# Causal attention in a hybrid block: key tiles in groups of four with the values one group later, and denominators from a sum in two float32r parts

## The chip, the cores and the metric

The kernel runs as one program on one core of a Trainium2 chip. The metric is the time of one execution on the device in microseconds (us). The names of the engines are those of the profile: PE is the matrix engine (PEld its weight loads), DVE the vector engine, ACT the scalar engine, POOL the general-purpose engine, SP the engine whose queue starts nearly all transfers (DMA) here.

## What is computed

One layer of a streaming encoder over 16 learned tokens and 2048 frames of width 1024, in float32. Three groups of heads read the same normalised input through one projection: a gated linear recurrence, eight heads of forgetting attention with 64 columns each, and a second recurrence (four heads, chunks of 64 frames). Their outputs are joined, projected, added to the input, and a gated feed-forward layer follows. The change concerns the attention alone:

```python
log_f = jax.nn.log_sigmoid(f_logit + f_bias)
c = jnp.cumsum(log_f, axis=1).transpose(0, 2, 1)
...
s = einsum('bhqd,bhkd->bhqk', qb, kh) + (cb[..., :, None] - c[..., None, :])
s = jnp.where(kpos[None, :] <= qpos[:, None], s, -jnp.inf)
p = jax.nn.softmax(s, axis=-1)
o = jnp.einsum('bhqk,bhkd->bhqd', p, vh)
```

## The kernel before

The program goes through the input projection with the recurrences beside it, then the attention (class `Attn`), the output projection (`w_out_tile`, tile `pswo`), and the feed-forward layer (tiles `psu`, then `psd`). All of the code's instructions are put in order for each engine by a scheduler that runs when the kernel is built; each engine then works through its own list strictly in that order, and so does SP's queue of transfers. The order of an engine is therefore no copy of the order of the code, but the code's order is what the scheduler starts from, and `issue_after` and `add_manual_dep` bind it.

`Attn.run` works in steps. A step is one head `h` and one block `b` of 512 queries; half 1 takes the blocks 0 and 1 of all heads, half 2 the blocks 2 and 3, so there are 32 steps. The keys of a step are cut into tiles of 128: a step of block b has 4b + 5 tiles (5, 9, 13 or 17), of which four lie on the diagonal and get narrower (512, 400, 272, 144 columns), and one has 16 rows only. For a tile,

- two float32r products make the transposed scores in tile `sc` (lines 623 and 624, two buffers in PSUM),
- ACT takes the exponential into tile `p` (line 626, `NP` = 5 buffers), and on the diagonal POOL masks it (`affine_select`, line 628),
- a product in plain float32 multiplies `p` by the values `v` into `po` (line 635). Two tiles make a pair: the one writes rows 0 to 63 of `po` and the other rows 64 to 127 (`tile_position`), and the first of them is made to wait for both exponentials,
- POOL, and for each fourth tile DVE, adds `p` into `acc` (line 656), one addition after the other; `acc` has two buffers, one for a step.

Before a step's scores, its maxima are needed (`maxima`): up to 20 products into `mx` (line 503), each reduced by DVE (line 506). They are for the step two ahead and are put between the pairs by `fill`, as are the tiles of the output projection that can already be made. At a step's end, `po` is read out (lines 664 to 667). The denominators follow in three parts, 2, 7 and 12 pairs later (`DELAYS`, `tick`): `total` adds the rows of `acc` by a plain float32 product with a column of ones (line 675), ACT writes the sum over row 0 of `acc` (line 676), and SP sends it out and back as a 16 x 32 tile; `invert` takes the reciprocal and sends it out and back again; `scale` multiplies. The eight w_out tiles 9 to 16 need the outputs of half 2's steps, and most of them run after the attention.

`keys` starts the loads of a head's keys and values. In half 2 a head fills one of two sets of buffers.

Of the kernel before, what the change touches and what calls it, by code (L numbers as in the profile page):

```python
# [18 lines left out]
P = 128  # L19
# [296 lines left out]
def attn_consts(core):  # L316
# [16 lines left out]
    core.ones_col = c.tile([P, 1], F32, name="ones_col")  # L333
    nc.vector.memset(core.ones_col[:], 1.0)
# [59 lines left out]
class Attn:  # L394
# [7 lines left out]
    def __init__(self, core, pool, psum, more, scr):  # L402
# [3 lines left out]
        self.clock, self.later, self.serial, self.added = 0, [], 0, 0  # L406

# [46 lines left out]
    def keys(self, h, nt):  # L454
# [20 lines left out]
        nc.sync.dma_start(v1[:, : nt - 1], scr["v"][: n - META, r].rearrange("(j p) d -> p j d", p=P))  # L475
        nc.sync.dma_start(v1[:META, nt - 1], scr["v"][n - META : n, r])
# [120 lines left out]
    def weights(self, h, b, keys, queries, fill):  # L597
# [4 lines left out]

        nc, core, scr = self.nc, self.core, self.scr
# [8 lines left out]
        po = self.psum.tile([P, 512], F32, tag="pv", name=core.n("po"), bufs=1)  # L612
        acc = self.t([P, 512], "acc")
        for jj in range(0, len(kt), 2):
            if jj:
                fill(min(1.0, (jj + 2) / len(kt)))
            self.tick()
            pair = kt[jj : jj + 2]
            ps_, exps = [], []
            for j, rows, c0, mw, mo in pair:  # L620
                w, ks = n - c0, P * j
                ps = self.ps("sc", 2)
                nc.tensor.matmul(ps[:rows, :w], k1[:, ks : ks + rows], q1[:, c0:n], start=True, stop=False)
                nc.tensor.matmul(ps[:rows, :w], k2[:, ks : ks + rows], q2[:, c0:n], start=False, stop=True)  # L624
                p = self.pool.tile([P, 512], F32, tag="p", name=core.n("p"), bufs=self.NP)
                last = nc.scalar.activation(p[:rows, :w], ps[:rows, :w], AF.Exp, bias=bias[:rows, j : j + 1])  # L626
                if mw:
                    last = nc.gpsimd.affine_select(
                        out=p[:rows, :mw], in_=p[:rows, :mw], compare_op=ALU.is_ge, fill=0.0, base=mo,
                        pattern=[[1, mw]], channel_multiplier=-1,  # L630
                    )
                ps_.append(p)
                exps.append(last)
            for i, (p, (j, rows, c0, mw, mo)) in enumerate(zip(ps_, pair)):
                mm = nc.tensor.matmul(
                    po[64 * i : 64 * i + 64, c0:n], v1[:rows, j], p[:rows, : n - c0],
                    start=jj == 0, stop=jj + i + 2 >= len(kt), tile_position=(0, 64 * i),
                )
                self.last = mm
                if i == 0 and len(pair) == 2:  # L640
                    core.tc.add_manual_dep(
                        mm.ins, exps[1].ins.name,
                        mybir.DependencyInfo(mybir.DependencyClass.Sync, mybir.DependencyReason.DATA),
                        reason="both of a pair at the same time",
                    )
            for i, (p, (j, rows, c0, mw, mo)) in enumerate(zip(ps_, pair)):
                if jj == 0 and i == 0:

                    c1 = pair[1][2] if len(pair) == 2 else n
                    if c1:  # L650
                        nc.gpsimd.tensor_copy(acc[:rows, :c1], p[:rows, :c1])
                    continue
# [3 lines left out]
                eng.tensor_tensor(a, ps_[0][:rows, c0:n] if jj == 0 else a, p[:rows, : n - c0], op=ALU.add)  # L656


        while len(self.later) > 8:
            self.later.pop(0)[2]()  # L660

        o, oh = self.t([64, 512], "o", bufs=4), self.t([64, 512], "oh")
        c1 = kt[1][2]
        nc.scalar.activation(oh[:, c1:n], po[64:128, c1:n], AF.Copy)
        if c1:
            nc.scalar.activation(o[:, :c1], po[0:64, :c1], AF.Copy)
        nc.vector.tensor_tensor(o[:, c1:n], po[0:64, c1:n], oh[:, c1:n], op=ALU.add)
        g = n // 16
        dcol = self.t([16, 32], "dcol", bufs=4)
        rows = kt[0][1]  # L670
        rb = []

        def total():
            ps = self.mx()
            nc.tensor.matmul(ps[0:1, :n], core.ones_col[:rows], acc[:rows, :n], start=True, stop=True)
            nc.scalar.activation(acc[0:1, :n], ps[0:1, :n], AF.Copy)
            nc.sync.dma_start(scr["den"][h : h + 1, ts], acc[0:1, :n])
            nc.sync.dma_start(dcol[:, :g], scr["den"][h, ts].rearrange("(p c) -> p c", c=g))

        def invert():  # L680
            rb.append(self.t([64, 512], "rb"))
            nc.vector.reciprocal(dcol[:, :g], dcol[:, :g])
            nc.sync.dma_start(scr["rden"][h, ts].rearrange("(p c) -> p c", c=g), dcol[:, :g])
            nc.sync.dma_start(rb[0][:, :n], scr["rden"][h : h + 1, ts].broadcast_to([64, n]))

        def scale():
            nc.vector.tensor_tensor(o[:, :n], o[:, :n], rb[0][:, :n], op=ALU.mult)
# [1375 lines left out]
```

## Time and profile before

| what | us |
|---|---|
| median of three runs (3157.63 to 3165.91) | 3165.64 |
| the profiled execution, its own time | 3168.61 |
| its span, first to last instruction | 3166.9 |
| input projection with recurrences, to the first scores | about 0 to 927 |
| attention, half 1, with the rest of the recurrences | about 927 to 1210 |
| attention, half 2, with parts of the output projection | about 1210 to 1690 |
| the rest of the output projection | about 1690 to 1800 |
| feed-forward layer | about 1800 to 3167 |

The bounds of the stages are the first and last starts of their instructions in the trace. Of the lines below, a row of a group of instructions gives the line of the code, the engine, the operation, the tiles it writes and reads, the shape and the count; then the busy time and the mean ns of one; then how long the engine stood idle before them, and which engine's work ended that. A row of stretches gives the busy time of each engine in that stretch (with the number of instructions), the granted clock of PE as a share of the full one, the share of the DMA engines and GB/s. PE's products overlap in time: what one costs is the distance from its start to the start of the next.

### The profile page before, as it was taken

To read this page: it belongs to the slowest core of one execution; us is meant where nothing else is said; L and a number is where in the kernel's file an instruction comes from. 1 tells how busy PE (TensorE), PEld (TensorE's weight loads), DVE (VectorE), ACT (ScalarE), POOL (GpSimd) and SP (SyncE) were. 2 spreads that over 40 slices of the span, in tenths; PEclk is the share of its full clock that TensorE was granted. 3 is DMA by queue.
4 is the path that set the end of the run, shared out by engine and by line. 5 is a ranking of instruction groups with operands and counts; after the bars stand their busy time and mean duration, and the time that the engine had idled before them with its cause. 6 is when DMAs were issued, how large, how long until landed. Compare 5 with 4: busy or idle time off the path is not lost. (4 is left out here: it accounts for less than half of the span.)

```text
span 3166.9 us, 52619 instructions
## 1 busy us (share of the span) xinstructions
PE 2955.7 (93%) x18488; PEld 2473.9 (78%) x18488; DVE 2196.1 (69%) x4563; ACT 1446.3 (46%) x2684; POOL 1274.0 (40%) x1426
## 2 busy tenths in 40 slices
PE   6988899999989998999999899999999999999998
PEld 6977788889965554554457699999999999787776
DVE  6147665766677777766657777787778787557777
ACT  3134323444444443434543456666666665324332
POOL 3334334211013444434651235433533334556665
PEclk9989899999987998999999899999999999999999
DMA  6777756643453344444326365555555565535444
GB/s 194 225 235 229 220 181 215 200 125 111 116 126 68 81 100 123 119 109 116 77 61 206 115 190 168 167 173 168 165 165 164 168 189 159 177 103 170 140 160 140
DMA packets 493817, 484.11 MB, mean 153 GB/s; under 512 B 83200, under 2 KB 408010, under 8 KB 487904
## 3 DMA queue, kind: packets, MB, share of 16 engines
q1 hardware_dynamic: 493168, 480.36, 50.8%
q8 instruction: 145, 2.38, 0.3%
q14 instruction: 120, 0.98, 0.1%
q0 software_dynamic: 384, 0.39, 0.0%
HBM read 354.76 MB, written 125.87 MB: 152 GB/s over the span
## 5 line engine op out<-in xcount | busy, mean ns | idle before, releaser
L150 PE MATMUL psu<-xo,uw 128*128 128x344 f32 x1848 | 588.7, 323 | 7.9 <-DVE wx L1413 4.8
L151 PE MATMUL psu<-xo,uw 128*128 128x344 f32 x1848 | 593.7, 322 | 1.0 <-DVE xo L1485 1.0
L152 PE MATMUL psu<-xo,uw 128*128 128x344 f32 x1848 | 583.0, 320 | 0.0
L150 PE MATMUL psp<-xh,wh 128*128 128x384 f32 (+2 forms) x1152 | 386.0, 335 | 0.0
L152 PE MATMUL psp<-xh,wl 128*128 128x384 f32 (+2 forms) x1152 | 382.1, 332 | 3.0 <-DVE wl L145 3.0
L151 PE MATMUL psp<-xl,wh 128*128 128x384 f32 (+2 forms) x1152 | 383.0, 332 | 0.0
L150 PEld LDWEIGHTS psu<-xo,uw 128*128 128x128 f32 x1848 | 347.5, 189 | 9.4 <-DVE wx L1413 5.2
L151 PEld LDWEIGHTS psu<-xo,uw 128*128 128x128 f32 x1848 | 348.9, 189 | 1.3 <-DVE xo L1485 1.3
L152 PEld LDWEIGHTS psu<-xo,uw 128*128 128x128 f32 x1848 | 347.2, 189 | 0.0
L1484 ACT ACTIVATE uw<-uq 128x512 fp32r<-128x512 f32 x462 | 287.0, 627 | 99.1 <-PE psu L152 48.0
L1485 DVE TENSOR_TENSOR uw<-uq,uw 128x512 fp32r<-128x512 f32 x330 | 283.2, 862 | 63.5 <-ACT uw L1484 58.6
L626 ACT ACTIVATE p<-sc,bias 128x512 f32<-128x512 f32 (+4 forms) x352 | 201.1, 592 | 267.8 <-PE sc L624 211.7
L1485 POOL TENSOR_TENSOR uw<-uq,uw 128x512 fp32r<-128x512 f32 x132 | 182.4, 1382 | 267.2 <-ACT uw L1484 233.8
L656 POOL TENSOR_TENSOR acc<-acc,p 128x512 f32<-128x512 f32 (+3 forms) x208 | 226.6, 1090 | 153.2 <-ACT p L626 118.8
L1584 DVE SCALAR_TENSOR_TENSOR uy<-psu,ffn_cols,uy 128x342 f32<-128x342 f32 (+1 forms) x396 | 224.2, 569 | 90.0 <-ACT uy L1582 88.9
L1590 POOL TENSOR_TENSOR uy<-uy,uy 128x342 f32<-128x342 f32 (+1 forms) x132 | 137.0, 1038 | 322.0 <-DVE uy L1584 133.9
L506 DVE TENSOR_REDUCE mc<-mx 128x1 f32<-128x400 f32 (+6 forms) x320 | 172.5, 554 | 93.4 <-PE mx L503 89.2
L152 PEld LDWEIGHTS psp<-xh,wl 128*128 128x128 f32 x1152 | 222.6, 193 | 10.3 <-issue 4.5
L150 PEld LDWEIGHTS psp<-xh,wh 128*128 128x128 f32 x1152 | 222.6, 193 | 8.8 <-issue 6.5
L151 PEld LDWEIGHTS psp<-xl,wh 128*128 128x128 f32 x1152 | 222.6, 193 | 6.5 <-issue 4.6
L1503 POOL TENSOR_TENSOR us<-us 128x512 f32<-128x512 f32 x88 | 131.3, 1492 | 222.3 <-DMA us<-in_ffn_up_dram 197.5
L1484 ACT ACTIVATE fo<-u 128x896 fp32r<-128x896 f32 x88 | 81.1, 922 | 234.3 <-POOL u L1700 117.1
(447 smaller groups left out, 6513.7 us busy)
## 6 DMA issues: line engine op xcount, KB each, us to landing
uq<-scr_us SPq DMA_DIRECT2D x264, 256.0 KB
uq<-in_ffn_up_dram SPq DMA_DIRECT2D x198, 256.0 KB
raw<-in_w_in_dram SPq DMA_DIRECT2D x72, 512.0 KB
us<-in_ffn_up_dram SPq DMA_DIRECT2D x44, 512.0 KB
scr_us<-us SPq DMA_DIRECT2D x22, 1024.0 KB
u<-scr_ff SPq DMA_DIRECT2D x88, 256.0 KB
scr_ff<-uy SPq DMA_DIRECT2D x110, 171.0 KB
q<-scr_qh SPq DMA_DIRECT2D x96, 128.0 KB
```

The lines of the kernel that those rows point to most:

```text
L150: nc.tensor.matmul(out, ah, bh, start=first, stop=False, skip_group_check=more)
L151: nc.tensor.matmul(out, ah, bl, start=False, stop=False, skip_group_check=more)
L152: nc.tensor.matmul(out, al, bh, start=False, stop=last, skip_group_check=more)
L506: self.reduced = nc.vector.tensor_reduce(mc[:rows, i, ci : ci + 1], ps[:rows, :full], axis=AX.X, op=ALU.max)
L626: last = nc.scalar.activation(p[:rows, :w], ps[:rows, :w], AF.Exp, bias=bias[:rows, j : j + 1])
L656: eng.tensor_tensor(a, ps_[0][:rows, c0:n] if jj == 0 else a, p[:rows, : n - c0], op=ALU.add)
L1484: core.nc.scalar.activation(hi, src, AF.Copy)
L1485: (eng or core.nc.vector).tensor_tensor(lo, src, hi, op=ALU.subtract)
L1503: add, sub = (lambda o, x, y, op=op: nc.gpsimd.tensor_tensor(o, x, y, op=op) for op in (ALU.add, ALU.subtract))
L1584: stt(y[:, :n], src[:, i : n + i], cw[:, 44 * i + cc : 44 * i + cc + 1], y[:, :n], op0=ALU.mult, op1=ALU.add)
L1590: core.pooled = nc.gpsimd.tensor_tensor(v[:, :n], g[:, :n], v[:, :n], op=ALU.mult)
```

## The change

The score products of four key tiles (`GROUP`; the last tile, with 16 rows, joins the last group) are issued before the value products of the group before them. `group_values` is kept in `pending` and called by `flush` after the next group's `group_scores`, in the next step if need be, and `issue_after(self.scored.ins)` holds each value product behind the last score product issued so far. `p` gets 9 buffers in place of 5. The loads of the values move behind that call too. In `total`, the sum of `acc` is split: ACT copies it rounded to float32r (`ah`), POOL subtracts that from `acc` (`al`), and two float32r products with the ones take the place of the plain float32 one. `ah` and `al` use the two buffers of tile `oh`. `total` now reads all 128 rows.

```diff
-    core.ones_col = c.tile([P, 1], F32, name="ones_col")
+    core.ones_col = c.tile([P, 1], F32R, name="ones_col")
...
-        nc.sync.dma_start(v1[:, : nt - 1], scr["v"][: n - META, r].rearrange("(j p) d -> p j d", p=P))
-        nc.sync.dma_start(v1[:META, nt - 1], scr["v"][n - META : n, r])
+        def values():
+            nc.sync.dma_start(v1[:, : nt - 1], scr["v"][: n - META, r].rearrange("(j p) d -> p j d", p=P))
+            nc.sync.dma_start(v1[:META, nt - 1], scr["v"][n - META : n, r])
+        self.loads.append(values)
...
+        groups = [kt[g : g + self.GROUP] for g in range(0, len(kt) - 1, self.GROUP)]
+        groups[-1].append(kt[-1])
...
+        def group_scores(group):
...
+            for jj in range(0, len(group), 2):
+                if done:
+                    fill(min(1.0, (done + 2) / len(kt)))
+                done += 2
+                self.tick()
+                for j, rows, c0, mw, mo in group[jj : jj + 2]:
...
+                    self.scored = nc.tensor.matmul(
+                        ps[:rows, :w], k2[:, ks : ks + rows], q2[:, c0:n], start=False, stop=True
+                    )
...
+        def group_values(group, ps_, start, end):
...
+            for i, ((p, _), (j, rows, c0, mw, mo)) in enumerate(zip(ps_, group)):
+                at = 64 * (i % 2)
+                with core.tc.issue_after(self.scored.ins):
+                    mm = nc.tensor.matmul(
+                        po[at : at + 64, c0:n], v1[:rows, j], p[:rows, : n - c0], start=start and i < 2,
+                        stop=end and i + 2 >= len(group), tile_position=(0, at),
+                    )
...
+            if end:
+                self.steps.append(self.last)
+                ending(po, acc)
...
-            ps = self.mx()
-            nc.tensor.matmul(ps[0:1, :n], core.ones_col[:rows], acc[:rows, :n], start=True, stop=True)
+                ah, al = (self.t([P, 512], "oh", F32R) for _ in range(2))
+                nc.scalar.activation(ah[:, :n], acc[:, :n], AF.Copy)
+                nc.gpsimd.tensor_tensor(al[:, :n], acc[:, :n], ah[:, :n], op=ALU.subtract)
+                ps = self.mx()
+                nc.tensor.matmul(ps[0:1, :n], core.ones_col[:], ah[:, :n], start=True, stop=False)
+                nc.tensor.matmul(ps[0:1, :n], core.ones_col[:], al[:, :n], start=False, stop=True)
...
+        for i, group in enumerate(groups):
+            ps_ = group_scores(group)
+            self.flush()
+            self.pending = lambda a=(group, ps_, i == 0, i == len(groups) - 1): group_values(*a)
+
+    def flush(self):
+        if self.pending:
+            self.pending()
+        self.pending = None
+        while self.loads:
+            self.loads.pop(0)()
+
+    GROUP = 4
-    NP = 5
+    NP = 9
```

The lines of `acc` and of the pairs' waiting are the same work as before with other indices; `ending` holds what stood at the end of `weights`. In the changed file the scores are lines 635 and 636, the exponential 640, the mask 642, the value product 658, the additions 679, the copy `ah` 702, the subtraction 703, the two sums 705 and 706, the maxima 509.

How PE's list changes, in the middle of a long step of half 2 (block 3, head 5; `sc` scores, `mx` maxima, `po` values). Before:

```order
L635 MATMUL po_15254<-p_15318,v_1500_10990 64x512
L635 MATMUL po_15254<-p_15323,v_1500_10990 64x512
L623 MATMUL sc_15342<-q_2704_14874,k_1498_10988 128x512
L624 MATMUL sc_15342<-q_1497_10986,k_1499_10989 128x512
L503 MATMUL mx_15329<-k_1494_10978,q_1491_10971 128x512
L623 MATMUL sc_15359<-q_2704_14874,k_1498_10988 128x512
L624 MATMUL sc_15359<-q_1497_10986,k_1499_10989 128x512
L503 MATMUL mx_15309<-k_1494_10978,q_1491_10971 128x400
L503 MATMUL mx_15351<-k_1494_10978,q_1491_10971 128x400
L635 MATMUL po_15254<-p_15340,v_1500_10990 64x512
L635 MATMUL po_15254<-p_15345,v_1500_10990 64x512
```

PE's list after, in the same step:

```order
L658 MATMUL po_15469<-p_15434,v_1500_10990 64x512
L658 MATMUL po_15469<-p_15439,v_1500_10990 64x512
L658 MATMUL po_15469<-p_15462,v_1500_10990 64x512
L658 MATMUL po_15469<-p_15467,v_1500_10990 64x512
L509 MATMUL mx_15444<-k_1494_10978,q_1491_10971 128x384
L635 MATMUL sc_15528<-q_2746_14970,k_1498_10988 128x512
L636 MATMUL sc_15528<-q_1497_10986,k_1499_10989 128x512
L635 MATMUL sc_15534<-q_2746_14970,k_1498_10988 128x400
L636 MATMUL sc_15534<-q_1497_10986,k_1499_10989 128x400
L509 MATMUL mx_15478<-k_1494_10978,q_1491_10971 128x400
L509 MATMUL mx_15428<-k_1494_10978,q_1491_10971 128x512
L509 MATMUL mx_15481<-k_1494_10978,q_1491_10971 128x512
```

Value products came in twos between scores; now they come in fours (or fives) with the scores and maxima of a whole group between. In the whole attention, value products stand in 174 unbroken rows before and in 93 after; rows of plain float32 products of any kind (values, denominators, transposes, small products of the recurrences) number 263 before and 172 after.

PE's list at a denominator sum (`ones_col`), a little earlier in that step, before:

```order
L623 MATMUL sc_15320<-q_2704_14874,k_1498_10988 128x512
L624 MATMUL sc_15320<-q_1497_10986,k_1499_10989 128x512
L675 MATMUL mx_15290<-acc_15081,ones_col 1x512
L623 MATMUL sc_15337<-q_2704_14874,k_1498_10988 128x512
L624 MATMUL sc_15337<-q_1497_10986,k_1499_10989 128x512
```

And after, near the end of the step:

```order
L635 MATMUL sc_15552<-q_2746_14970,k_1498_10988 128x144
L636 MATMUL sc_15552<-q_1497_10986,k_1499_10989 128x144
L705 MATMUL mx_15453<-oh_15449,ones_col 1x512
L706 MATMUL mx_15453<-oh_15450,ones_col 1x512
L635 MATMUL sc_15566<-q_2746_14970,k_1498_10988 16x16
L636 MATMUL sc_15566<-q_1497_10986,k_1499_10989 16x16
```

One float32 product between scores became two float32r ones, and they stand farther behind the end of the step whose sum they make.

POOL's list at the end of a step (`acc_15081` belongs to the step that ends, `acc_15255` to the next), before:

```order
L628 AFFINE_SELECT p_15212<-p_15212 128x128
L656 TENSOR_TENSOR acc_15081<-acc_15081,p_15196 128x400
L628 AFFINE_SELECT p_15218<-p_15218 128x128
L656 TENSOR_TENSOR acc_15081<-acc_15081,p_15212 128x272
L628 AFFINE_SELECT p_15236<-p_15236 16x16
L656 TENSOR_TENSOR acc_15081<-acc_15081,p_15218 128x144
L656 TENSOR_TENSOR acc_15255<-p_15259,p_15264 128x512
```

POOL's list after, at the end of the same step (there `acc_15291`, and `acc_15470` the next):

```order
L642 AFFINE_SELECT p_15318<-p_15318 128x128
L642 AFFINE_SELECT p_15330<-p_15330 128x128
L642 AFFINE_SELECT p_15336<-p_15336 128x128
L642 AFFINE_SELECT p_15346<-p_15346 16x16
L679 TENSOR_TENSOR acc_15291<-acc_15291,p_15318 128x400
L679 TENSOR_TENSOR acc_15291<-acc_15291,p_15330 128x272
L679 TENSOR_TENSOR acc_15291<-acc_15291,p_15336 128x144
L703 TENSOR_TENSOR oh_15450<-acc_15291,oh_15449 128x512
L679 TENSOR_TENSOR acc_15470<-p_15368,p_15373 128x512
```

The masks moved ahead of the additions, and the subtraction stands between the last addition of one step and the first of the next. It reads `oh_15449`, which ACT makes four exponentials behind the step's last one.

More of the change, by code (lines that the diff above doesn't have):

```diff
@@ L611, in weights @@
         ts = slice(t0, t0 + n)
[L612 to L630, printed above, removed]
-                    )
[L632 to L638, printed above, removed]
@@ L655, in weights @@
                 a = acc[:rows, c0:n]
[L656 to L667, printed above, removed]
```

85 lines of the change are left out of this document (56 added, 29 removed).

## The prediction

> **What bounds the kernel now.** I read the page's head first, for where the span goes, and then a table of stretches, which splits the stage that the change touches. For each engine it gives the busy time and in brackets the instructions; behind these stand the granted clock of PE, the DMA share and GB/s.
>
> ```profile
> PE 2955.7 (93%) x18488; PEld 2473.9 (78%) x18488; DVE 2196.1 (69%) x4563; ACT 1446.3 (46%) x2684; POOL 1274.0 (40%) x1426
> ...
> 927.00:1210.00 283.00, 259.04 (x2254) 160.85 (x2254) 214.31 (x699) 123.59 (x265) 113.97 (x206) 0.86 0.39 92
> 1210.00:1500.00 290.00, 263.77 (x1066) 146.34 (x1064) 209.45 (x532) 121.82 (x210) 124.74 (x139) 0.94 0.47 119
> 1500.00:1620.00 120.00, 115.08 (x464) 53.64 (x463) 83.86 (x195) 61.70 (x103) 79.05 (x92) 0.98 0.33 74
> 1620.00:1690.00 70.00, 68.63 (x290) 43.30 (x291) 29.29 (x79) 26.20 (x50) 24.40 (x30) 1.00 0.22 66
> 1690.00:1800.00 110.00, 89.83 (x398) 72.94 (x396) 85.04 (x206) 40.78 (x73) 21.51 (x18) 0.91 0.55 184
> ```
>
> PE is the bound of the program, and of the attention too: in half 2 (1210 to 1690) it is busy 263.8 + 115.1 + 68.6 = 447.5 of 480 us, 93%. In half 1 the recurrences run beside it: PE is busy 92%, but at a clock of 0.86, and DVE 76%. The lists after differ from those before only between the first value product and the end of the attention, apart from a few neighbours changed further on. So a gain or a loss arises in these 760 us, and what follows is work of PE again and passes it on.
>
> The view that prices the change is PE's timeline, since what a product costs is the distance to the next start (first column; the second is the time until its end, the last bracket idle time).
>
> ```profile
> 1407.74 1.02 PE L675 MATMUL mx<-acc,ones_col 128*1 128x512 f32 x2 [0.87 <-DVE mc L506]
> 1408.69 0.50 PE L623 MATMUL sc<-q,k 128*128 128x512 f32 x1
> 1409.03 0.40 PE L624 MATMUL sc<-q,k 128*128 128x512 f32 x1
> 1409.27 0.39 PE L503 MATMUL mx<-k,q 128*128 128x512 f32 x1
> 1409.50 0.39 PE L623 MATMUL sc<-q,k 128*128 128x512 f32 x1
> 1409.72 0.40 PE L624 MATMUL sc<-q,k 128*128 128x512 f32 x1
> 1410.05 1.94 PE L635 MATMUL po<-p,v 128*64 128x512 f32 x8
> 1411.92 0.73 PE L503 MATMUL mx<-k,q 128*128 128x512 f32 x2
> 1412.48 0.40 PE L623 MATMUL sc<-q,k 128*128 128x512 f32 x1
> ...
> 1413.24 1.08 PE L635 MATMUL po<-p,v 128*64 128x512 f32 x4
> 1414.25 0.51 PE L623 MATMUL sc<-q,k 128*128 128x512 f32 x1
> 1414.59 0.40 PE L624 MATMUL sc<-q,k 128*128 128x512 f32 x1
> 1414.82 0.39 PE L150 MATMUL pswo<-woh,mh 128*128 128x512 f32 x1
> ```
>
> A float32r product of 512 columns costs 0.23 us (1409.27 to 1409.50). A pair of value products, four records, costs 1.01 (1413.24 to 1414.25), two pairs in a row 1.87 (1410.05 to 1411.92). The neighbours pay too: the last product ahead of a row of values takes 0.33 (1409.72 to 1410.05), 0.10 more than usual, and the first behind it 0.34 (1414.25 to 1414.59), 0.11 more. A lone pair thus costs 0.10 + 1.01 + 0.11 = 1.22, two joined 0.10 + 1.87 + 0.10 = 2.07, since the two maxima behind them take 0.56 in place of 0.46. **Joining two rows of values saves 2.44 - 2.07 = 0.37 us.**
>
> The denominator's product in float32 takes 0.95 (1407.74 to 1408.69), and the one behind it again 0.11 more: it is charged for like a row of values.
>
> **The change, part by part.**
>
> *Fewer rows.* Counted in the lists, plain float32 products stand in 103 unbroken rows in half 1 before and 83 after, in half 2 in 153 and 86. That is 20 x 0.37 = 7.4 us in half 1 and 67 x 0.37 = 24.8 us in half 2.
>
> The Trainium skill, page "TensorEngine Tiling (Array Packing)", section "Key Properties", says that changing the tiling mode drains the engine. By that rule only the value products, which use half the columns, would pay: 174 - 93 = 81 joints, 81 x 0.37 = 30.0 us, where the rows of all float32 products give 32.2. The row at 1408.69, behind a product that isn't tiled by hand, shows the same surcharge, so I keep the rows of float32.
>
> *Denominators.*
>
> ```profile
> L675 PE MATMUL mx<-acc,ones_col x64: 588/591/1057, 999.8 to 1682.6; 128*1 128x512 f32 x64
> ```
>
> 64 records are 32 products of two passes; by the list 13 lie in half 1 and 19 in half 2. A pass inside a row costs 0.43 (1.87 less the two ends, 0.15, over four; the ends are what 1.01 has above two such passes). Two float32r products cost 0.46, so each saves 0.86 - 0.46 = 0.40: 5.2 us in half 1, 7.6 us in half 2. In sum PE gets rid of 12.6 us in half 1 and 32.4 in half 2.
>
> *Added on ACT and POOL.* A copy and a subtraction of 128 x 512 for each of the 32 sums; the nearest rows are the splits of the weights.
>
> ```profile
> L1484 ACT ACTIVATE uw<-uq 128x512 fp32r<-128x512 f32 x462 | 287.0, 627 | 99.1 <-PE psu L152 48.0
> L1485 POOL TENSOR_TENSOR uw<-uq,uw 128x512 fp32r<-128x512 f32 x132 | 182.4, 1382 | 267.2 <-ACT uw L1484 233.8
> ```
>
> That is 0.63 us on ACT and 1.38 on POOL a step. ACT is busy 61.7 of 120 us and has room. For POOL the additions matter, which form one chain with DVE's.
>
> ```profile
> L656 POOL TENSOR_TENSOR acc<-acc,p 128x512 f32<-128x512 f32 x38 | 49.3, 1298 | 34.6 <-ACT p L626 33.4
> L656 DVE TENSOR_TENSOR acc<-acc,p 128x512 f32<-128x512 f32 x15 | 10.3, 687 | 5.1 <-POOL acc L656 4.5 <-POOL p L628 0.6
> L656 POOL TENSOR_TENSOR acc<-p,p 128x512 f32<-128x512 f32 x6 | 7.7, 1280 | 4.1 <-ACT p L626 4.1
> ```
>
> These are of 1500 to 1620, where no output projection runs. Six first additions mean six steps, so 20 us a step; POOL's 79.05 us are 13.2 a step, DVE's additions 10.3 / 6 = 1.7, waiting between the two 4.5 / 6 = 0.75. With the subtraction (1.38) and ACT's copy ahead of it (0.63), for which POOL now waits between two steps, the chain is 13.2 + 1.7 + 0.75 + 1.38 + 0.63 = 17.7 us. PE would need 20 - 32.4 / 16 = 18.0. The two are nearly level. The upper end of the chain is 18.5, if the copy waits for one more exponential (0.69). PE's gain of half 2 is then between 16 x 1.5 = 24 us and, at the 93% that PE is busy, 0.93 x 32.4 = 30 us. I take the middle, 27.
>
> *Half 1.* What bounds it is mixed: DVE 76%, PE at a clock of 0.86, and POOL waits for a free `acc` there:
>
> ```profile
> POOL acc L656 <- DMA scr_den<-acc: 42.2, 6, 14.8
> ...
> ACT p L626 <- POOL acc L656: 19.9, 14, 4.8
> ```
>
> (Of the whole attention: time in all, times, the longest.) An `acc` is freed a group later than before, four tiles, and `p` has four more buffers, so the two offset each other. Between nothing and 12.6 I take 5 us.
>
> *Moved: values behind a group of scores.* A pair waited for two exponentials that had just begun; now they are long done, so PE's waiting for ACT there goes. What waits instead is the fifth, sixth and further score tile for one of two `sc` buffers. Per group of four PE has 8 x 0.23 of scores, 1.87 + 0.2 of values and some four maxima, 0.9, together 4.8 us, and ACT four exponentials, 2.8 us, by the row of 1500 to 1620:
>
> ```profile
> L626 ACT ACTIVATE p<-sc,bias 128x512 f32<-128x512 f32 x66 | 44.5, 687 | 47.5 <-PE sc L624 29.5 <-PE po L635 13.4 <-POOL acc L656 3.8
> ```
>
>  Two of them fit beside the values, the next two beside two scores and maxima. I cost this at nothing; the cover is gone where maxima run out, and then it is some 0.2 us a group, 80 groups, 16 us. The other way, the waits that go are worth up to
>
> ```profile
> PE sc L623 <- ACT p L626: 5.2, 8, 2.1
> PE po L635 <- ACT p L626: 3.7, 4, 2.9
> PEld sc L623 <- ACT p L626: 38.2, 60, 2.5
> ```
>
> 9 us by PE's own rows, and 20 if half of what the weight loads waited counts. Both go into the range.
>
> *Moved: the loads of the values*, 32 transfers of SP's queue, now behind the first group of the next step. Their user comes two steps later, 36 us, so nothing waits. The sums' transfers sit at the head of SP's queue until ACT has written (in all 75.9 us in the attention); keys and queries stand behind them, and PE waited 11.4 us for keys:
>
> ```profile
> SPq L677 <- ACT acc L676: 75.9, 20, 9.4
> PE mx L503 <- DMA k<-scr_cl: 11.4, 4, 4.4
> ```
>
> The chain ahead of that wait grows by 0.63 + 1.38 - 0.40, about 1.6 us; the list puts the sums later by as much or more. I cost it at nothing; at worst four waits of 1.6 more, 6 us.
>
> *The end.* Behind the last value product the same 1.6 us stand, under the output projection that by the list still follows, 360 products of 0.23, 83 us. Nothing.
>
> **Sum:** 27 + 5 = 32 us. The profiled execution took 3168.61 (span 3166.9), 3.0 above the median of 3165.64. 3168.61 - 32 = 3136.6, so 3133.6 against the median; I say 3134.
>
> **Rivals.**
>
> *The waits go too* (3100). PE's 45.0 us count fully, and 20 us of waits for exponentials go: 3165.6 - 65 = 3100. For it speaks that `p` with 9 buffers lets POOL fall back by twice as much before ACT stops; against it that DVE and POOL are at 70% and 66% in 1500 to 1620 and would be at about 80%, where new waits arise.
>
> *The clock eats the gain* (3153). The granted clock falls where PE pauses:
>
> ```profile
> 980.00:1000.00 20.00, 20.00 (x124) 11.29 (x123) 9.56 (x25) 5.00 (x11) 5.61 (x9) 0.67 0.06 11
> ...
> 1240.00:1260.00 20.00, 14.17 (x52) 5.89 (x50) 14.07 (x21) 8.55 (x12) 11.41 (x8) 0.83 0.68 195
> 1260.00:1280.00 20.00, 20.00 (x87) 9.12 (x86) 18.03 (x37) 11.52 (x21) 11.99 (x12) 1.00 0.45 142
> ```
>
> Half 2's mean, 0.96 over its three stretches, is some 20 us of lost clock in 480. If pauses behind the two `sc` buffers bring it to 0.92, 19 us more go, and 13 us of gain are left: 3153. The Trainium skill, page "TensorE: Matmul & The Clock Gate", section "A second HAM failure mode: psum-queue depth-cycling", tells of just that: small pauses between groups that cycle through PSUM buffers make the clock fall back to half. Against it: 1500 to 1620, where scores wait for two buffers already, holds 0.98.
>
> *POOL becomes the bound* (3180, slower). The list puts a step's masks ahead of additions that are ready, and the subtraction ahead of the next step's first addition. If POOL stands idle while the diagonal exponentials come in, three gaps of 1.2 us (18.0 over 15 tiles), 3.6 us, the chain is 17.7 + 3.6 = 21.3 a step, 1.3 more than now; 16 steps give 20 us, and with half 1 losing what it could gain (5) the loss is about 15 to 25: 3180 to 3190. It decides from 20 us a step on. Then the copy `ah` on ACT waits for POOL with the exponentials queued behind it, and PE for `sc`. Against it: only some steps have masks ahead of more than one ready addition, and POOL's free time there was 5 us a step.
>
> **Chances.** The forecast, 3112 to 3150: 0.62. Waits go too, below 3112: 0.12. Clock, or POOL level with PE, 3150 to 3165: 0.16. POOL or the queues make it slower than before: 0.10. What a measurement can tell from no change is 0.3%, 9.5 us: 3156 to 3175. Of the third case a third lies below 3156, and two thirds within; of the last a fifth within. Faster 0.62 + 0.12 + 0.05 = 0.79, same 0.11 + 0.02 = 0.13, slower 0.08. The range takes in half of the second case and nearly all of the third: 3102 to 3161.
>
> **What the profile after would show.** PE's sum of distances in 927 to 1690 down by some 45 us; pairs at 0.93 in rows of eight records and more; the sums as two float32r products 0.46 apart in all; no row of ACT waiting for POOL's additions above 20 us; POOL busy near 80% where no output projection runs; the attention's last value product at about 1650 in place of 1682, and the stretches behind it unchanged. The forecast is wrong if POOL's waits for the copy `ah`, or ACT's for `acc`, come to more than 2 us a step, if the granted clock of half 2 falls below 0.92, or if half 1 takes longer than now.

## The result, and the profile after

The changed kernel took 3131.33 us in the median of 4 runs (3124.71 to 3138.93), the kernel before 3165.77 (3157.63 to 3166.46): a ratio of 0.9898, with an interval of 0.9871 to 0.9924. The forecast was 3134 (3102 to 3161). Run again beside a later measurement of the kernel before, the changed kernel came to 3136.28 against 3170.59, 0.9882 (0.9855 to 0.9908). The gain is 34 us, and 32 were forecast.

The first line of the page, and then a table of stretches cut at the kernel's own marks. The first stretch goes from the first score to the first product `mx<-mq,mk` of the learned tokens (half 1), the second to the last value product (half 2), the third to the first product of the first feed-forward stage (the output projection that is left). The columns are those of the prediction's table. The changed kernel:

```profile
PE 2938.6 (94%) x18488; PEld 2504.0 (80%) x18488; DVE 2218.7 (71%) x4563; ACT 1456.5 (46%) x2716; POOL 1320.1 (42%) x1458
...
915.00:1195.00 280.00, 255.23 (x2158) 174.97 (x2158) 220.54 (x686) 125.00 (x268) 133.20 (x215) 0.80 0.39 93
1195.00:1648.00 453.00, 426.59 (x1853) 254.30 (x1852) 331.17 (x803) 214.86 (x383) 259.15 (x282) 0.96 0.40 104
1648.00:1759.00 111.00, 94.05 (x431) 75.14 (x430) 83.57 (x213) 36.57 (x70) 20.77 (x18) 0.96 0.56 183
```

The kernel before, cut the same way:

```profile
927.00:1203.00 276.00, 252.22 (x2190) 157.41 (x2190) 211.01 (x686) 120.38 (x259) 113.73 (x205) 0.86 0.40 94
1203.00:1682.00 479.00, 446.30 (x1848) 240.99 (x1847) 320.76 (x803) 210.70 (x363) 228.43 (x260) 0.96 0.40 100
1682.00:1791.00 109.00, 91.56 (x405) 72.93 (x405) 82.69 (x208) 35.00 (x67) 20.20 (x17) 0.93 0.53 177
```

Half 2 went from 479 to 453 us, and nothing else got shorter: half 1 from 276 to 280, the rest of the output projection from 109 to 111. In half 2 PE's busy time fell by 19.7 us and its idle time (length less busy time) from 32.7 to 26.4. The clock there is 0.96 as before; in half 1 it went from 0.86 to 0.80. From the first score to the last value product it is 734 us now against 755.

The two profiled executions differ in one more place. The attention begins at 927 us before and at 915 after, 12 us of the 33 between them. That isn't the change: a second profile of each kernel (below) has 920 before and 921 after. From the first score to the first product of the feed-forward layer it is 864 us before and 844 after in this pair of profiles, 871 and 839 in the second, so 20 and 32 us.

PE's timeline, with a joined row, a denominator and a wait (columns as in the prediction):

```profile
1501.74 0.40 PE L636 MATMUL sc<-q,k 128*128 128x512 f32 x1
1502.07 1.94 PE L658 MATMUL po<-p,v 128*64 128x512 f32 x8
1503.94 0.69 PE L509 MATMUL mx<-k,q 128*128 128x512 f32 x2
1504.46 0.40 PE L635 MATMUL sc<-q,k 128*128 128x512 f32 x1
...
1506.76 0.40 PE L705 MATMUL mx<-oh,ones_col 128*1 128x512 f32 x1
1507.00 0.39 PE L706 MATMUL mx<-oh,ones_col 128*1 128x512 f32 x1
1507.23 0.17 PE L635 MATMUL sc<-q,k 128*16 128x16 f32 x1
...
1511.96 0.49 PE L635 MATMUL sc<-q,k 128*128 128x512 f32 x1 [0.20 <-ACT p L640]
```

Two pairs in one row: 0.33 ahead, 1.87 inside, 0.52 for the two maxima behind. The denominator is two products, 1506.76 to 1507.23, 0.47 us in all, with no surcharge on a neighbour. And the scores of a group's fourth tile wait 0.20 us for an exponential, which is to say for one of the two `sc` buffers: the wait that the prediction had costed at nothing.

### The profile page after: what moved, and what is told of

Its sections match the earlier page's. It is cut to its first block, busy times and chain, and to the rows that moved or that the text cites. A ratio compares the mean times of both kernels' runs of the same rounds, so it can differ in the third digit from the quotient of the medians.

```text
span 3134.1 us, 52572 instructions
## 1 busy us (share of the span) xinstructions
PE 2938.6 (94%) x18488; PEld 2504.0 (80%) x18488; DVE 2218.7 (71%) x4563; ACT 1456.5 (46%) x2716; POOL 1320.1 (42%) x1458
## 5 line engine op out<-in xcount | busy, mean ns | idle before, releaser
L679 POOL TENSOR_TENSOR acc<-acc,p 128x512 f32<-128x512 f32 (+3 forms) x208 | 229.4, 1105 | 91.3 <-ACT p L640 35.4
L512 DVE TENSOR_REDUCE mc<-mx 128x1 f32<-128x400 f32 (+5 forms) x320 | 172.2, 554 | 61.9 <-PE mx L509 57.3
L1529 DVE TENSOR_TENSOR fo<-u,fo 128x896 fp32r<-128x896 f32 x88 | 107.0, 1216 | 116.5 <-ACT fo L1528 116.5
```

The lines of the kernel that those rows point to most:

```text
L512: self.reduced = nc.vector.tensor_reduce(mc[:rows, i, ci : ci + 1], ps[:rows, :full], axis=AX.X, op=ALU.max)
L679: eng.tensor_tensor(a, ps_[0][0][:rows, c0:n] if start and i == 1 else a, p[:rows, : n - c0], op=ALU.add)
L1529: (eng or core.nc.vector).tensor_tensor(lo, src, hi, op=ALU.subtract)
```

## The experiments

All ratios are against the kernel before on the same chip. PE's numbers are of half 2 in each kernel's profile, cut as above; a row is an unbroken row of plain float32 products, counted in the trace. The lengths of the halves are from the starts in the trace (453.8 for the stretch of 453 above); busy and idle come from stretches cut at whole microseconds.

| kernel | ratio (95%) | half 1 | half 2 | PE busy | PE idle | rows |
|---|---|---|---|---|---|---|
| before | | 276 | 479 | 446.3 | 32.7 | 153 |
| before again | 0.9994 (0.9980-1.0007) | 277 | 486 | 451.1 | 35.9 | 153 |
| changed | 0.9898 (0.9871-0.9924) | 280 | 454 | 426.6 | 26.4 | 86 |
| changed again | 0.9882 (0.9855-0.9908) | 274 | 454 | 427.0 | 27.1 | 86 |
| nine buffers only | 0.9967 (0.9952-0.9981) | 274 | 473 | 441.1 | 31.9 | 153 |
| denominators only | 1.0050 (1.0030-1.0069) | 294 | 484 | 445.4 | 38.6 | 140 |
| groups, plain sums | 0.9913 (0.9892-0.9934) | 272 | 458 | 430.7 | 27.3 | 94 |
| groups of two | 0.9912 (0.9894-0.9930) | 285 | 456 | 441.7 | 14.3 | 134 |
| groups of two, plain sums | 0.9927 (0.9902-0.9953) | 285 | 461 | 445.8 | 14.2 | 146 |
| rows broken again | 1.0004 (0.9987-1.0022) | 282 | 459 | 427.5 | 31.5 | 150 |
| subtraction made twice | 0.9907 (0.9886-0.9928) | 275 | 457 | 427.9 | 29.1 | 80 |
| subtraction on DVE | 0.9963 (0.9951-0.9975) | 281 | 464 | 428.4 | 35.6 | 84 |
| plain sums in half 1 only | 0.9946 (0.9930-0.9963) | 283 | 462 | 434.3 | 27.7 | 89 |
| three `sc` buffers, two `mx` | 1.0152 (1.0128-1.0177) | 285 | 500 | 428.1 | 71.9 | 78 |

**Both kernels again**, unchanged, as a floor for all that follows.

> The kernel before once more, for a second profile of it. In the first one the attention's first score came at 927 us, in the changed kernel's at 915, though nothing ahead of it is changed. Theory (that is chance): here the first score comes somewhere from 912 to 930 and the distance from the first score to the feed-forward layer's first product is again 864 within 6 us; 3158 to 3168 in time. Rival (the difference is a consequence of the change): 927 again within 2 us.

> The changed kernel once more, on the same chip as the other three, and for a second profile. Theory: 0.988 to 0.992 of before; first score to first product of the feed-forward layer 844 within 6 us, half 1 280 within 4 us. Rival (half 1's 280 was a chance of that execution): half 1 at 272 and 836 in all.

Measured: before again 3168.34 us against 3171.42; changed again 3136.28 against 3170.59. The profiles of one and the same kernel differ by 7 us in half 2 (before) and by 6 in half 1 (changed, 274, nearer to the rival's 272 than to 280). A difference of that size in a single profile proves nothing.

**The two parts apart.** Denominators alone (in the kernel before):

```
+            ah, al = (self.t([P, 512], "oh", F32R) for _ in range(2))
+            nc.scalar.activation(ah[:, :n], acc[:, :n], AF.Copy)
+            nc.gpsimd.tensor_tensor(al[:, :n], acc[:, :n], ah[:, :n], op=ALU.subtract)
...
-            nc.tensor.matmul(ps[0:1, :n], core.ones_col[:rows], acc[:rows, :n], start=True, stop=True)
+            nc.tensor.matmul(ps[0:1, :n], core.ones_col[:], ah[:, :n], start=True, stop=False)
+            nc.tensor.matmul(ps[0:1, :n], core.ones_col[:], al[:, :n], start=False, stop=True)
```

> The kernel before with only the denominators made from two float32r parts. Theory: 13 rows fewer (250 against 263), 13 x 0.37 = 5 us, and 32 x 0.40 = 13 us of passes, of which the larger part of half 2's 12 us remains: 8 to 15 us faster than before, about 3154. Rival (waits): POOL's subtraction lengthens the chain of additions with only five buffers of p, and that eats it: 3163 to 3172.

Groups alone (the same lines taken out of the changed kernel):

> The changed kernel with the denominators' plain float32 product put back; the groups of four stay. Theory (fewer rows): its list has 184 rows of plain float32 products against 263 before, 79 x 0.37 = 29 us less for PE, 21 of them in half 2; half 1 keeps little, since its clock falls; so 18 to 29 us faster than before, about 3143. Rival (waits): the gain is that values no longer wait for fresh exponentials and that p has nine buffers, the sums add nothing: as fast as the changed kernel, 3131.

Measured: denominators alone 3185.68 against 3171.42, 14 us slower, which neither expectation had; groups alone 3142.19, 29 us faster, at the upper end of what was expected. The loss lies in half 1, and this is what POOL waited for there, in the kernel with the denominators alone (time in all, times, longest):

```profile
POOL oh L676 <- DVE sh L516: 11.9, 1, 11.9
POOL oh L676 <- PE sc L624: 9.3, 1, 9.3
...
POOL oh L676 <- ACT oh L675: 6.8, 4, 4.2
```

L676 is the subtraction. It sits in POOL's queue and waits, through ACT's copy, for engines that work on other things (`sh`, scores), and the masks and additions queued behind it wait with it: with its smaller waits some 33 us. In the changed kernel the same waits come to about 20 in half 1. That these waits are the loss isn't shown. The tables of half 1, of the kernel before in its second profile and of the denominators alone:

```profile
920.00:1197.00 277.00, 253.03 (x2190) 157.88 (x2190) 210.86 (x684) 120.68 (x259) 113.94 (x205) 0.86 0.40 93
921.00:1215.00 294.00, 269.33 (x2184) 173.85 (x2184) 223.34 (x686) 127.42 (x271) 127.57 (x219) 0.77 0.38 88
```

PE is idle for 24 us in the one and 25 in the other. The 17 us are busy time at a clock of 0.77 in place of 0.86, which is some 29 us more of lost clock, and what lowered it stays open. What follows: the two-part sum was no gain by itself. Beside groups of four its share is the step from 0.9913 to 0.9898 or 0.9882, with intervals that overlap.

**Nine buffers alone** (`NP = 9` in the kernel before):

> The kernel before with nine buffers of p in place of five, nothing else. Theory (the waits that groups of two took away, from 47 to 26 us in half 2, went because values come late): waits stay at 45 to 50 and half 2 at 478 to 487; same time as before within 5 us. Rival (they went because p has more buffers): waits fall to some 30, half 2 at 462, 3150.

Measured: 3157.79 against 3166.56, 9 us faster, with half 2 at 474: between the two expectations. So a quarter of the whole gain needs no group at all. What ACT waited for in the attention, where the kernel before has 23.4 us in the first of these rows and 19.9 in the second:

```profile
ACT p L626 <- PE po L635: 1.2, 1, 1.2
ACT p L626 <- POOL acc L656: 9.4, 3, 7.9
```

Both are exponentials that wait for a free `p`.

**Groups of two**, `GROUP = 2` in place of 4, with and without the two-part sums:

> The changed kernel with groups of two: values still come behind the scores of the next group, p has nine buffers, the sums are in two parts, but the list has 230 rows of plain float32 products (172 with groups of four, 263 before). Theory (fewer rows): 33 x 0.37 + 13 = 25 us less for PE, some 15 of them in half 2; 10 to 20 us faster than before, 3146 to 3156. Rival (waits): the lateness of the values is what counts, and it is there: 3131, as with groups of four.

> The changed kernel with groups of two and the plain float32 sum: of the change only the lateness of the values and the nine buffers are left, the list has 254 rows against 263 before. Theory (lateness takes away some 20 us of waits in half 2, the two-part sums give nothing in time): as fast as groups of two with two-part sums, 25 to 30 us faster than before. Rival (the two-part sums carry part of what groups of two gained): only 10 to 18 us faster than before.

Measured: 3140.98 against 3171.42 and 3150.54 against 3170.59, 30 and 20 us faster. The first is more than the theory of fewer rows allows; the second lies between its two expectations. These kernels hardly join rows: 134 and 146 are left of 153 in half 2. They only multiply the values a group later. So buffers and lateness, with hardly a joint, are worth some 20 us. The table of stretches of groups of two, half 2:

```profile
1199.00:1655.00 456.00, 441.67 (x1891) 252.42 (x1892) 335.82 (x817) 217.93 (x388) 250.46 (x278) 0.95 0.42 105
```

PE is idle for 14.3 us. With groups of four it is busy 15 us less and idle 12 us more. What PE waited for says where these come from. Groups of two, half 2:

```profile
PE sc L635 <- ACT p L640: 3.5, 3, 3.2
PE mx L509 <- DVE mc L512: 3.0, 4, 1.2
...
PE mx L509 <- DVE mc L515: 0.4, 1, 0.4
```

Groups of four (the changed kernel), half 2:

```profile
PE mx L509 <- DVE mc L512: 8.9, 7, 3.5
PE sc L635 <- ACT p L640: 5.6, 13, 1.4
PE mx L509 <- DVE mc L515: 3.9, 4, 2.4
```

These three rows hold 18.4 us of waits against 6.9. I read them so: a group of four asks for more score and maximum tiles in a row than there are buffers, and part of the gain by joined rows is turned into these waits. (Groups of two also have 39 more output-projection products inside half 2, 9.0 us of the 15 at 0.23 each; they are missing behind it, where 106 us are left in place of 111.)

**Rows broken again.** The changed kernel with its groups, buffers and sums, and a float32r product of 16 columns, which nothing reads, between the pairs of a group (`ones_r` are 16 columns of ones):

```
+                if i % 2 == 0 and i:
+                    with core.tc.issue_after(self.last.ins):
+                        between = nc.tensor.matmul(
+                            self.mx()[0:1, :16], core.ones_col[:], core.ones_r[:], start=True, stop=True
+                        )
-                with core.tc.issue_after(self.scored.ins):
+                with core.tc.issue_after(between.ins if i > 1 else self.scored.ins):
```

> The changed kernel with a float32r product of 16 columns, into a buffer that nobody reads, between any two pairs of values of a group: values come as late as in the changed kernel, but the list has 258 rows of plain float32 products in place of 172. Theory (joined rows are worth 0.37 us each on PE's path): 86 x 0.37 = 32 us more for PE, 24 of them in half 2, and some 5 us for 112 small products; 20 to 35 us slower than the changed kernel. Rival (lateness is what pays; joints are swallowed by waits): at most 10 us slower than the changed kernel.

Measured: 3175.31 us against 3170.59, and the changed kernel beside it 3136.28: 39 us slower than that, all of the gain gone and more than the 20 to 35 expected. Its timeline at a broken row:

```profile
1508.01 1.08 PE L665 MATMUL po<-p,v 128*64 128x512 f32 x4
1509.02 0.17 PE L661 MATMUL mx<-ones_r,ones_col 128*1 128x16 f32 x1
1509.12 1.08 PE L665 MATMUL po<-p,v 128*64 128x512 f32 x4
1510.13 0.73 PE L511 MATMUL mx<-k,q 128*128 128x512 f32 x2
```

From 1508.01 to 1510.13 are 2.12 us where the joined row takes 1.87: the break costs 0.25, of which 0.03 is the small product itself (by the changed kernel's products of 16 columns). Its table of stretches, half 2 and the output projection left behind it:

```profile
1208.00:1667.00 459.00, 427.53 (x1855) 234.65 (x1853) 319.81 (x779) 212.84 (x375) 262.89 (x284) 0.96 0.39 99
1667.00:1798.00 131.00, 110.27 (x492) 89.04 (x492) 92.30 (x236) 39.85 (x77) 20.41 (x18) 0.95 0.51 167
```

PE is busy as long as in the changed kernel, but does 63 output-projection products fewer, 14.5 us at 0.23, which then stand behind the attention (131 us there, 20 more). So 64 more rows go with some 15 us of PE in half 2, 0.24 each, and 5 us more idle time; the small products also take `mx` buffers, and PE waited 6 us for those in half 2.

But the edit changed more than the joints. Of the 79 small products in half 2 only 26 stand between two value products as above; 52 stand behind a score, a maximum or another wide product, which the scheduler now puts between the pairs of a group. So the second pair also comes later, and exponentials wait for a free `p` again:

```profile
ACT p L642 <- PE po L665: 27.4, 17, 3.9
ACT p L642 <- PE mx L661: 22.6, 10, 10.1
```

In half 2 the first of these was 22.9 us in the kernel before and 1.2 in the changed one. PE also waits 9.1 us for keys there, where the changed kernel has 1.4. What follows: four late pairs that are not joined, as this list has them, are no faster than the kernel before. What the joints alone are worth this run doesn't show; the 39 us are an upper end, since the other waits are in them.

**POOL's load.** The subtraction made twice (the same line repeated, into the same tile), and made on DVE (`nc.vector` in place of `nc.gpsimd`):

> The changed kernel with POOL's subtraction made twice, 1.38 us more on POOL for each of 32 sums. Theory of the prediction (POOL's chain is level with PE in half 2): 16 x 1.38 = 22 us slower than the changed kernel. Rival (POOL has room behind nine buffers): within 5 us of the changed kernel.

> The changed kernel with the subtraction on DVE in place of POOL. Theory (POOL's waiting ahead of the subtraction is what costs in half 1): half 1 at 270 to 276 us; in half 2 POOL's chain is 1.38 us a step shorter and DVE's work 0.7 longer, 450 to 456; 5 to 10 us faster than the changed kernel. Rival (any engine that takes the subtraction blocks its queue, DVE worse than POOL, since the recurrences and the maxima stand behind it): half 1 at 280 to 290, no faster than the changed kernel.

Measured: made twice 3143.61 against 3170.59, 7 us slower than the changed kernel beside it (the intervals of the two ratios overlap), with half 2 at 457: nearer to the rival's 5 than to the theory's 22. The table of stretches, half 2:

```profile
1199.00:1656.00 457.00, 427.89 (x1840) 256.90 (x1839) 343.39 (x802) 214.59 (x381) 285.02 (x301) 0.95 0.41 103
```

POOL is busy 26 us more than in the changed kernel, and the half is 3 us longer. POOL's chain isn't level with PE. On DVE the subtraction was worse, as the rival had it: 3153.95 against 3166.56, 0.9963, with half 2 at 464 (half 1, 281, is as long as in one profile of the changed kernel). Three waits that the changed kernel has at 3.7, 10.3 and 5.6 us, the first two of the whole attention, the last of half 2:

```profile
POOL acc L679 <- DMA scr_den<-acc: 98.2, 16, 21.3
...
ACT p L640 <- POOL acc L679: 43.7, 27, 6.5
...
PE sc L635 <- ACT p L640: 16.7, 17, 4.5
```

They read as one chain: POOL runs ahead to the next sum and stands at a tile `acc` that the last sum's transfer hasn't freed, exponentials wait for its additions, and scores for exponentials. By this reading, which no run tests, the time that POOL spends on the subtraction is time in which that transfer gets done, and an engine with less to do waited longer.

**Plain sums in half 1 only** (blocks 0 and 1 keep the float32 product, the others the two-part sum), for the theory that the subtraction at the head of POOL's queue is what keeps half 1 from gaining:

> The changed kernel, but the steps of half 1 (blocks 0 and 1) keep the plain float32 sum; half 2 keeps the two float32r parts. Theory (POOL's subtraction stands at the head of POOL's queue in half 1, in front of the recurrences' steps, and PE's clock falls while they are late): half 1, from the first score to the product of the learned tokens, takes 272 us in place of 280 to 285, half 2 stays at 454; 5 to 12 us faster than the changed kernel, 3120 to 3135 against before at 3170. Rival (half 1's clock is chance): half 1 between 278 and 286, no change to the changed kernel, 3135 to 3140.

Measured: 3149.91 against 3166.56, 0.9946: slower than the changed kernel, half 1 at 283. The theory falls. Half 2, where this kernel computes what the changed one does, was 8 us longer too: the scheduler's list shifts with any edit, and shifts of this size are not to be explained by the edit.

**A third `sc` buffer.** The scores get the PSUM buffer that the maxima shared, so that a group's later scores need not wait:

```
+        return self.ps("mx", 2)
+
+    def sc(self):
...
-            return self.more.tile([P, 512], F32, tag="mx", name=self.core.n("mx"), bufs=1)
+            return self.more.tile([P, 512], F32, tag="mx", name=self.core.n("sc"), bufs=1)
-        return self.ps("mx", 2)
+        return self.ps("sc", 2)
...
-                    ps = self.ps("sc", 2)
+                    ps = self.sc()
```

> The changed kernel with the third shared PSUM buffer given to the scores in place of the maxima (scores three, maxima two). Theory (with groups of four PE's remaining 42 us of waits in half 2 are scores waiting for one of two buffers): waits fall to some 25 us, half 2 from 454 to 438, 3120 against before at 3170. Rival (they are maxima waiting for DVE): the waits move to the maxima, half 2 at 454 to 465.

Measured: 3212.18 against 3166.56, 1.0152, far from both expectations. Half 2 took 500 us at a clock of 0.91:

```profile
1209.00:1709.00 500.00, 428.14 (x1730) 248.76 (x1730) 307.79 (x751) 208.37 (x369) 251.46 (x278) 0.91 0.36 90
```

What PE waited for there:

```profile
PE sc L639 <- ACT p L644: 14.8, 17, 3.1
...
PE mx L513 <- DVE q L542: 11.5, 8, 4.3
PE mx L513 <- DVE mc L519: 9.5, 6, 2.5
PE mx L531 <- DVE mc L506: 7.3, 6, 1.3
PE mx L513 <- DVE mc L516: 7.1, 11, 1.2
```

Four rows of the tile `mx`, 35.4 us, and scores waiting for exponentials longer than with two buffers (14.8 us against 5.6). I read it so that the third buffer is worth more to the maxima, where PE stops first. No version was faster than the changed kernel.

## Why the prediction was right, point by point

*Joining two rows saves 0.37.* The price stands. In the changed kernel's trace rows of eight records take 0.33 ahead, 1.87 inside and 0.34 behind, as predicted, and over 63 rows of all lengths at full clock the neighbours' surcharge has medians of 0.10 and 0.11 (worked out from the starts in the trace). A row broken by a small product costs 0.25, less than 0.37: 0.15 of it is inside the rows (two of 1.01 in place of one of 1.87), and the small product takes 0.10, where two wide neighbours pay 0.21 more. That a float32 sum, which isn't tiled by hand, also counts as a row is borne out by the 0.47 of its two float32r products without any surcharge.

*PE gets rid of 32.4 us in half 2.* Right as to the work, but part of it came back. The rows went from 153 to 86, as the list said, and the busy time from 446.3 or 451.1 to 427, by 20 to 24 us. The distances between starts, less idle time, show what is in it (two profiles of each kernel). The products next to a row were dearer than the same products elsewhere by 30.2 and 31.5 us, and are now by 17.7 and 17.6. The value products went from 119.8 and 121.0 to 113.6 and 115.0 with nine or ten more of them in the half, 8 us less at the same number. The sums went from 17.9 and 18.4 to 8.7 and 8.8. That is 30 to 32 us, so the 32.4 are there. Besides, 24 output-projection products (5.5 us) left the half, and values and small products of the recurrences, 5 to 6 us, came in over its border. What the prediction did not count are 8 to 10 us at products that mostly stand away from the rows: 52 products in place of 35 are followed by an idle time and so take their full length, and others keep a longer distance without any idle time. I take these for short pauses that read as busy time.

*Waits at nothing.* The idle time of half 2 fell by 6 to 9 us, so this term was a gain. It is a difference of larger ones. What went is above all PE's wait for keys, 11.4 and 11.9 us in the two profiles of the kernel before; in the changed kernel it is

```profile
PE mx L509 <- DMA k<-scr_cl: 1.4, 2, 1.1
```

and nothing in its second profile. It is 9.7 us with nine buffers alone, and 0 and 3.2 with groups of two. The prediction had this wait in view and allowed for 6 us more of it, not for its end; why the keys now come in time (the later value loads, the later sums, or the list) no run separates. The value products' wait for exponentials, 3.7 us, went as it said. Against these, products into `mx` wait 13.1 us for DVE's maxima in place of 8.1, and scores 5.6 us for exponentials in place of 1.4. Groups of two show that lateness and buffers by themselves take idle time from 33 or 36 to 14 us, and four scores in a row bring it back to 26. The rival "the waits go too" thus came true for groups of two and half true here, as far as the waits go; the mechanism that the prediction put into its range (scores waiting for a buffer) is one of the two that show.

*Half 2 as 27.* Measured 25 to 32. Right in its sum, and put together otherwise: 20 to 24 of busy time and 6 to 9 of idle time, where I had cut PE's 32.4 down because POOL's chain would be nearly level. That the time came out within 3 us is thus luck in part: the reason for the cut was wrong, the pauses and the lost wait for keys weren't in the sum, and half 1's 5 us are not seen; these errors offset each other. How much of the 34 us the joined rows carry isn't settled either, since groups of two with plain sums gain 20 with hardly a joint.

*POOL's chain nearly level with PE.* Wrong. The step that failed is to lay all of a step's additions, subtraction and waits end to end and compare with PE's 18 us; with nine buffers POOL's work of one step overlaps the next, and 26 us more of it cost 3 in half 2, 7 in all. POOL reached 76% where no output projection runs, near the 80% named:

```profile
1460.00:1580.00 120.00, 112.67 (x485) 61.33 (x486) 94.95 (x222) 67.05 (x115) 91.77 (x102) 0.99 0.43 100
```

ACT's waits for POOL's additions, 19.9 us before, fell to

```profile
ACT p L640 <- POOL acc L679: 10.3, 8, 3.1
```

us in the attention. The rival "POOL becomes the bound" is out.

*Half 1 as 5.* Not seen: 276 and 277 before, 280 and 274 after. PE's rows became fewer there too (111 in the trace before, 96 after, 15 fewer where the lists had 20), and its busy time still went from 252 to 255 or 246, at a clock of 0.80 or 0.83 in place of 0.86. A mean clock of 0.80 over 280 us is 56 us of lost clock, 0.86 over 276 is 39. So the rival "the clock eats the gain" fits half 1, where I hadn't placed it, and was wrong on half 2, where I had (0.96 and 0.96 after, 0.96 and 0.94 before). The Trainium skill, page "TensorE: Matmul & The Clock Gate", section "A second HAM failure mode: psum-queue depth-cycling", has small pauses of groups that cycle through PSUM buffers bring the clock down; with three `sc` and two `mx` buffers half 2 fits that (0.91, with PE idle for 72 us), and with 26 us of idle time it does not show. PE's idle time alone doesn't give the clock: groups of two have 14 us of it in half 2 and 0.95, and of the rows that the prediction shows for pauses and clock the first has 0.67 with PE busy throughout. What lowers half 1's clock, in nearly all versions that move or add work, stays open; the subtraction on POOL alone is not it (groups of two with plain sums have none, and 0.80).

*Denominators, 12.8 us of passes.* The price holds (0.47 for the pair of products), the gain can't be told from nothing: 0.9913 without, 0.9898 and 0.9882 with. Left out of the sum was that the two-part sum can cost more than its own time: 14 us where there are no groups. Whether that comes from the subtraction's waits at the head of POOL's queue isn't shown.

*Value loads, SP's queue, the end.* No loss, as costed, but the wait for keys in half 2 turned into the gain told above; what stands behind the attention is the same but for the 24 products that moved there.

The attention's last value product came at 1648.4, where 1650 was named:

```profile
L658 PE MATMUL po<-p,v x704: 204/592/1116, 969.7 to 1648.4; 128*64 128x512 f32 x112, 128*64 128x272 f32 x19, 16*64 16x16 f32 x16, 128*64 128x400 f32 x16
```

Part of that agreement is chance, since the attention began 12 us earlier; in the second profile it began at 921 and ended at 1648.9.

*What the profile after would show.* Two of the signs that the prediction named against itself did appear. POOL's waits ahead of the subtraction come to 68.9 us over 32 steps, 2.2 a step, where it had set 2 (11.2 of them are put down to the copy's own end), without POOL's chain becoming the bound; and half 1 is longer in the first profile, though not in the second. PE's busy time of both halves fell by 17 us in the first pair of profiles and 31 in the second, where 45 were named.

## What to carry to other kernels

Products of different precision on one engine are priced by the unbroken row, so read what a switch costs from the distances to the neighbours, and count rows in the list. Then ask what the longer rows make wait, also by pauses that read as busy time: here 30 us of work went from half 2 and 20 to 24 of busy time, and groups of two, with hardly a row fewer, came within 4 to 10 us of groups of four. The own time of a new instruction on a side engine doesn't price it: the subtraction is 1.28 us, repeating it came out 7 us slower for 32 of them, and the two-part sums in the kernel without groups 14, with a lower clock in half 1 and no more idle time of PE there.

## What the hardware showed that I had not expected

A product of 16 columns takes 0.03 us among its like and 0.10 between two rows of plain float32, and a row that is broken by it pays 0.25 us, two thirds of what a wide product makes it pay.

Moving one PSUM buffer of five from the maxima to the scores cost 2.6 to 2.7% against the changed kernel (1.0152 over 0.9898 and 0.9882 is 1.0257 and 1.0273, by ratios): half 2 alone took 46 us longer, with PE idle for 72 us in place of 26 and the granted clock at 0.91 in place of 0.96. The list shifted with it: 59 fewer output-projection products stand in that half.
